# A hybrid decoder block on one core: queries loaded ahead, gate products dealt first and last, the residual through the weight tiles, the query projection in one block

## The chip, the cores and the metric

One core of a Trainium2 chip. The metric is the device time of one execution in microseconds (us); lower is better. The kernel before was timed three times.

## The reference, cut to what matters

All of it in float32: one sequence of 1024 tokens, width 1024, one layer.

```
h = rms_norm(x); proj = h @ w_in                      # q | six k/v parts | branch gates | pool input | merge gates
a = nsa_attention(q, kv, gates, ...) @ w_branch_attn   # compressed blocks, selected blocks, sliding window
b = pool_mixer(u_pool) @ w_branch_pool
ga, gb = split(sigmoid(g_merge))
x = x + (ga * a + gb * b) @ w_out                      # residual
x = x + square(relu(rms_norm(x) @ w_ff1)) @ w_ff2
return rms_norm(x)
```

With 16 selected blocks of 64 out of 16, the selected branch is plain causal attention. Eight heads of 64 in two groups share keys and values.

## The kernel before, in words

Every float32 matrix product is made of three products in TensorE's reduced float32 form: each operand is split into a high part (a cast on ScalarE, `hi`) and a low part (a subtraction on VectorE or GpSimd, `lo`), and `mm3` (lines 74 to 79) runs hi by hi, hi by lo and lo by hi for each block of 128 of the sum. A "term" below is one such triple.

`load` (lines 164 to 183) brings weights: a DMA on the SP queue into a raw tile `wraw` (four slots, `RAWS`), a cast to `whi` and a subtraction to `wlo` (three slots each, `HILO`), or, when a pool `blk` is given, into `bhi` and `blo`, which stay for a whole block of work.

The framework orders each engine's instructions itself ahead of time, by program order and by when it reckons that operands are there; on the chip each engine runs its list in that order. A pool that is opened where another was closed reuses its memory, and its tiles wait until the old ones are no longer read.

The stages, in program order:

1. Keys and values of the first parts (lines 229 to 271).
2. `block2` and `compress` (lines 286 to 384, called in lines 405 to 411): the rest of the keys and values, and the compressed blocks; `X`, `Xh`, `Xl` are the work tiles of `compress`.
3. `qblock(0)` and `qblock(1)` (lines 386 to 403): queries, 256 columns each, for eight tiles of 128 tokens. Each result is copied twice side by side by ScalarE (`q`, two slots), rotated by GpSimd (`rope`), and written to DRAM (`qd`). `keys` (lines 358 to 366) rotates and transposes keys in between, with `rope` on VectorE; both use the buffers `ropeA` and `ropeB` (two slots each).
4. The pool mixer and its gate `gb` (lines 424 to 505). Its weights' low parts are made by GpSimd. GpSimd also issues large DMAs that add weight blocks in DRAM for the MLP (`weight_sums`).
5. Attention (lines 511 to 744): 32 pairs of heads and token tiles (i from 0 to 7, four head pairs each). `units_a` is scores and softmax of a pair, `units_b` transposes the probabilities (`tr`) and multiplies them with the values (`pv`); they are interleaved, the `units_b` of one pair with the `units_a` of the next. The compressed values `vch` have 64 rows, all others (`vst`) 128. Between them, `advance` (lines 689 to 694) deals out 128 terms of the gate projection `ga` (`ga_terms`, PSUM tile `psG`), in proportion to the work done: `given < nterm * done / total`. The queries are read back from `qd` by `load_q` (lines 541 to 544) into `qi`, and transposed and split by `split_q`.
6. The merge (lines 787 to 825), in two halves of 512 tokens: for eight blocks, the attention branch's projection times `ta` (the gate from stage 5) plus `gb`, both read from DRAM; then eight blocks of `w_out`. The residual `xT` is written by DMA straight into `acc[:, m, sl]` (line 817), and line 820 adds to it.
7. The MLP with the norms (lines 829 to 984).

Of the kernel before, what the change touches and what calls it, by code (L numbers as in the profile page):

```python
# [49 lines left out]
def build(tc, a, out, dbg=None):  # L50
# [87 lines left out]

    def rope(eng, v, nh, cos, sin, wk):
        cb = cos[:, None, None, :].to_broadcast([P, nh, 2, 8])  # L140
        sb = sin[:, None, :].to_broadcast([P, nh, 8])
        A = wk.tile([P, 8, 2, 8], F32, name="ropeA", bufs=2)[:, :nh]
        B = wk.tile([P, 8, 2, 8], F32, name="ropeB", bufs=2)[:, :nh]
        x = v[:, :, 0:16].rearrange("p h (b e) -> p h b e", b=2)
        eng.tensor_tensor(A, x, cb, op=MUL)
        eng.tensor_tensor(B[:, :, 0], x[:, :, 1], sb, op=MUL)
        eng.tensor_tensor(B[:, :, 1], x[:, :, 0], sb, op=MUL)
        eng.tensor_tensor(x[:, :, 0], A[:, :, 0], B[:, :, 0], op=SUB)
        eng.tensor_tensor(x[:, :, 1], A[:, :, 1], B[:, :, 1], op=ADD)

# [13 lines left out]
    def load(src, lo_eng=None, blk=None):  # L164
# [3 lines left out]
        for a0 in range(0, na, step):  # L168
            w = step * n
            raw = strm.tile([P, HALF], F32, tag="wraw", name="wraw", bufs=RAWS)  # L170
            if blk is None:
                hi = strm.tile([P, HALF], F32R, tag="whi", name="whi", bufs=HILO)
                lo = strm.tile([P, HALF], F32R, tag="wlo", name="wlo", bufs=HILO)
            else:
                hi = blk.tile([P, 280], F32R, tag="bhi", name="bhi", bufs=10)
                lo = blk.tile([P, 280], F32R, tag="blo", name="blo", bufs=10)
            v, h, l = raw[:, :w], hi[:, :w], lo[:, :w]
            nc.sync.dma_start(v.rearrange("p (a n) -> p a n", a=step), src[:, a0:a0 + step, :])
            nc.scalar.copy(h, v)  # L179
            sub(lo_eng or nc.gpsimd, l, v, h)  # L180
            his.append(h.rearrange("p (a n) -> p a n", a=step))
            los.append(l.rearrange("p (a n) -> p a n", a=step))
# [4 lines left out]
    vst = [vk.tile([P, NT, NG, P], F32R, name=f"vst{b}") for b in range(2)]  # L187
    vch = vk.tile([DH, NG, P], F32R, name="vch")
    kds = vk.tile([P, NG, NCB + S], F32R, name="kds")
# [91 lines left out]
    with ExitStack() as st:  # L281
        psF = pool(st, "psF", bufs=4, space=PSUM)
        psH = pool(st, "psH", bufs=2, space=PSUM)
        wkA = pool(st, "wkA", side="right")

        def compress(kv):
            X = wkA.tile([P, 16, NG, NCB], F32, name="X")
            Xh = wkA.tile([P, 16, NG, NCB], F32R, name="Xh")
            Xl = wkA.tile([P, 16, NG, NCB], F32R, name="Xl")
            nc.gpsimd.memset(X[DH:P, :, :, NCB - 1:NCB], 0.0)  # L290
# [57 lines left out]
            else:  # L348
# [6 lines left out]
                for g in range(NG):  # L355
                    nc.vector.tensor_copy(vch[:, g], f(vh[g * DH:(g + 1) * DH]))

# [27 lines left out]

        def qblock(b):
            w = block_w(b * 256, 256)
            for t in range(NT):
                sl = slice(t * P, (t + 1) * P)
                ps = psF.tile([P, HALF], F32, name="psF")  # L390
                mm3(ps[:, :256], [(XH[k][:, sl], XL[k][:, sl], w[0][:, k], w[1][:, k])
                                  for k in range(NK)])
                q = wkA.tile([P, 4, 2, DH], F32, name="q", bufs=2)
                nc.scalar.activation(q, dup(ps[:, :256].rearrange("p (h d) -> p h d", d=DH)), AF.Copy,
                                     scale=req[:, t:t + 1])
                rope(nc.gpsimd, q.rearrange("p h e d -> p (h e) d"), 8, cosT[:, t], sinT[:, t], wkA)
                nc.sync.dma_start(qd[t][:, b * 512:(b + 1) * 512], q.rearrange("p h e d -> p (h e d)"))
                if b == 0:
                    keys(t, 0, kds[:, :, NCB + t * P:NCB + (t + 1) * P])
                elif t in (2, 5):  # L400
                    hf = t // 3
                    bcast(rB[:, hf * HALF:(hf + 1) * HALF], rcol[:, 4 * hf:4 * hf + 4],
                          psH.tile([P, HALF], F32, name="psH"), wkA)
# [7 lines left out]
        nc.vector.tensor_scalar(sg, sg, 0.5, 0.5, op0=MUL, op1=ADD)  # L411
        qblock(0)
        qblock(1)
        dump("kds", f(kds))
# [5 lines left out]
    kvctx.close()  # L420
    blkctx.close()


    with ExitStack() as st:
# [6 lines left out]
        with ExitStack() as st2:  # L431
# [45 lines left out]
            for m in (3, 2, 1, 0):  # L477
                cur = pool_in(m)
                if prev is not None:
                    pool_mix(*prev)  # L480
                prev = cur
            for m in range(NK):
                if made:
# [27 lines left out]
    with ExitStack() as st:  # L511
# [13 lines left out]
        def ga_terms():  # L525
            for m in range(NK):
                gh, gl = load(cols(a["w_in"], C_GA + m * P, P))
                for hf in range(2):
# [10 lines left out]
                    yield  # L539

        def load_q(i, g):
            qi = wk.tile([P, HALF], F32, name="qi", bufs=2)
            nc.sync.dma_start(qi, qd[i][:, g * HALF:(g + 1) * HALF])
            return qi

# [90 lines left out]
        def units_b(u):  # L636
            i, hp, g, nw, w0 = (u[n] for n in ("i", "hp", "g", "nw", "w0"))
            blocks = [(u["pS"], NCB + b * P, vst[0][:, b, g], P) for b in range(i + 1)]
            blocks += [(u["pW"], b * P, vst[1][:, w0 + b, g], P) for b in range(nw // P)]
            blocks.append((u["pS"], 0, vch[:, g], NCB))  # L640
            o = oacc[:, hp % 2]
# [4 lines left out]
            def tr(gi):  # L646
                bl = groups[gi]
                n = len(bl)
                ps = psT.tile([P, HALF], F32, name="psT").rearrange("p (b e n) -> p b e n", b=2, e=2)
                for j, (src, c0, _, _) in enumerate(bl):  # L650
                    for e in range(2):
# [7 lines left out]
            def pv(gi):  # L659
                ph, pl = parts.pop(gi)  # L660
                for part in (ph, pl):
                    for j, (_, _, v, rows) in enumerate(groups[gi]):
                        nc.tensor.matmul(o, lhsT=v, rhs=part[:rows, j], start=gi == 0 and j == 0 and part is ph,  # L663
                                         stop=2 * gi + j == nb - 1 and part is pl)
# [16 lines left out]

        LAG = 1
        fill = ga_terms()
        pairs = [(i, hp) for i in range(NT) for hp in range(NH // 2)]
        weight = [min(i + 1, 5) + i + 2 for i, _ in pairs]
        total, nterm = sum(weight), 2 * NK * NK
        done, given, summed = 0.0, 0, 0

        def advance(w):
            nonlocal done, given  # L690
            done += w
            while given < nterm and given < nterm * done / total:
                next(fill, None)
                given += 1

        qi = load_q(0, 0)
        q = split_q(qi)
        qnext = load_q(0, 1)
        bseq, bw = [], 0
# [42 lines left out]
        dump("oT", oT)  # L742
    psTctx.close()
    attn.close()

# [41 lines left out]
    with ExitStack() as st:  # L787
        wm = pool(st, "wm")
        for hf in range(2):
# [25 lines left out]
            for m in range(NK):  # L815
                wh, wl = load(cols(a["w_out"], m * P, P), nc.vector)
                nc.sync.dma_start(acc[:, m, sl], a["xT"][m * P:(m + 1) * P, sl])
                ps = bank()
                mm3(ps, [(wh[:, k], wl[:, k], mg[k][0], mg[k][1]) for k in range(NK)])
                nc.vector.scalar_tensor_tensor(acc[:, m, sl], ps, 0.5, acc[:, m, sl], op0=MUL, op1=ADD)  # L820
                square_into(sqs, acc[:, m, sl], m == NK - 1, sqa)
# [222 lines left out]
```

## Time and profile before

| | |
|---|---|
| median of 3 runs | 1493.94 us (1491.46 to 1497.39) |
| the profiled execution | 1493.06 us |
| its span, first to last instruction | 1491.3 us |
| TensorE busy | 1443.1 us (97%) |
| VectorE busy | 1006.1 us (67%) |
| ScalarE busy | 759.2 us (51%) |
| GpSimd busy | 154.1 us (10%) |

The profile is one execution. Times in it run from the span's start. Busy shares are of the span. A TensorE product is listed with its start and its own length; products overlap, so that the distance from one start to the next is what a product costs in a row of them.

### The profile page before, as it was taken

The page shows a single profiled execution, that of the slowest core. Times are in us where ns is not written, and L with a number is a line of the kernel's source. Part 1 is how long each engine was busy: PE and PEld are TensorE (multiplying, and loading weights), DVE is VectorE, ACT ScalarE, POOL GpSimd, SP SyncE. Part 2 cuts the span into 40 slices and gives each one's busy share as a digit, 9 for nine tenths or more (in the row PEclk, how much of TensorE's full clock was granted, in tenths as well). Part 3 has the DMA queues.
Part 4 walks back from the last instruction along what each step waited for, and adds up shares of the span by engine and source line. Part 5 has one row for each costly group of instructions (what it writes and reads, how often), then busy time and mean ns, then how long its engine had stood idle before and what let it go on. Part 6 is the DMA issues. An engine that isn't in the chain of part 4 may idle for free.

```text
span 1491.3 us, 20797 instructions
## 1 busy us (share of the span) xinstructions
PE 1443.1 (97%) x7385; PEld 1193.7 (80%) x7385; DVE 1006.1 (67%) x1950; ACT 759.2 (51%) x1559; POOL 154.1 (10%) x214
## 2 busy tenths in 40 slices
PE   8899999998999999999899999999999999999996
PEld 6788888886778887787688888888888888888885
DVE  5793461115888888787657658667897376669995
ACT  4454231124778877776334454575344454764451
POOL 2006423331111111111000000000000000000000
PEclk9999999999999999999999999999999999999998
DMA  8234217875768678766955332333233233333323
GB/s 309 69 100 149 71 43 189 215 202 132 201 156 212 153 187 196 171 169 150 327 174 162 108 97 91 100 100 99 85 106 97 94 99 93 99 94 97 98 80 113
DMA packets 130233, 204.67 MB, mean 137 GB/s; under 512 B 9936, under 2 KB 62928, under 8 KB 129616
## 3 DMA queue, kind: packets, MB, share of 16 engines
q1 hardware_dynamic: 112064, 136.22, 29.7%
q0 software_dynamic: 17920, 67.11, 19.9%
q8 instruction: 58, 0.95, 0.2%
q14 instruction: 47, 0.39, 0.1%
q10 hardware_dynamic: 144, 0.00, 0.0%
HBM read 186.52 MB, written 83.89 MB: 181 GB/s over the span
## 4 chain that ended last, share of the span: by engine, by line
PE 87%; DVE 5%; DMA 3%; ACT 2%; issue 1%; POOL 0%; SPq 0%; DVEq 0%; ACTq 0%; POOLq 0%
PE psm L79 16%; PE psm L77 16%; PE psm L78 16%; PE oacc L663 6%; PE psF L78 5%; PE psF L79 5%; PE psF L77 5%; PE psT L652 4%; PE psS L557 3%; PE psS L558 2%; PE psG L77 2%; PE psG L78 2%; PE psG L79 2%; DMA gb<-gbd 1%; PE psS L560 1%
## 5 line engine op out<-in xcount | busy, mean ns | idle before, releaser
L77 PE MATMUL psm<-mv,whi 128*128 128x512 f32 x896 | 350.6, 391 | 0.0
L78 PE MATMUL psm<-mv,whi 128*128 128x512 f32 x896 | 350.6, 391 | 0.0
L79 PE MATMUL psm<-mv,wlo 128*128 128x512 f32 x896 | 350.5, 391 | 0.0
L866 ACT CAST whi<-wraw 128x512 fp32r<-128x512 f32 x224 | 138.9, 621 | 257.6 <-PE psm L78 193.0
L82 DVE TENSOR_TENSOR wlo<-wraw,whi 128x512 fp32r<-128x512 f32 x288 | 196.7, 686 | 90.7 <-ACT whi L866 70.0
L78 PEld LDWEIGHTS psm<-mv,whi 128*128 128x128 f32 x896 | 168.3, 188 | 36.8
L77 PEld LDWEIGHTS psm<-mv,whi 128*128 128x128 f32 x896 | 168.3, 188 | 36.7
L79 PEld LDWEIGHTS psm<-mv,wlo 128*128 128x128 f32 x896 | 168.3, 188 | 36.7
L179 ACT CAST whi<-wraw 128x512 fp32r<-128x512 f32 x112 | 69.7, 622 | 122.2 <-PE psF L78 57.9
L656 DVE TENSOR_TENSOR pl<-psT,ph 128x512 fp32r<-128x512 f32 (+1 forms) x160 | 101.9, 646 | 30.3 <-ACT ph L655 29.0
L655 ACT CAST ph<-psT 128x512 fp32r<-128x512 f32 (+1 forms) x160 | 87.7, 556 | 49.4 <-PE psT L652 47.6
L567 DVE TENSOR_REDUCE nm<-psS 128x1 f32<-128x64 f32 (+8 forms) x192 | 99.8, 539 | 17.4 <-PE psS L560 10.2
L82 POOL TENSOR_TENSOR wlo<-wraw,whi 128x512 fp32r<-128x512 f32 x48 | 65.5, 1367 | 120.3 <-ACT whi L179 100.0
L77 PE MATMUL psF<-xh,whi 128*128 128x512 f32 x192 | 74.7, 389 | 0.0
L78 PE MATMUL psF<-xl,whi 128*128 128x512 f32 x192 | 74.7, 389 | 0.0
L79 PE MATMUL psF<-xh,wlo 128*128 128x512 f32 x192 | 74.7, 389 | 0.0
L568 ACT ACTIVATE pS<-psS,nm 128x64 f32<-128x64 f32 (+8 forms) x128 | 67.9, 532 | 8.8 <-DVE nm L567 8.3
L846 ACT CAST mv<-mt 128x512 fp32r<-128x512 f32 x96 | 59.1, 617 | 15.9 <-DVE mt L844 11.4
L82 DVE TENSOR_TENSOR mv<-mt,mv 128x512 fp32r<-128x512 f32 x96 | 65.0, 684 | 1.1 <-ACT mv L846 0.6
L663 PE MATMUL oacc<-ph,vst 128*128 128x256 f32 x264 | 64.0, 317 | 1.2 <-ACT ph L655 0.9
L652 PE MATMUL psT<-cf,pS 128*128 128x128 f32 x352 | 60.5, 276 | 2.7 <-DVE pS L624 2.6
L77 PE MATMUL psF<-bhi,xh 128*128 128x256 f32 (+1 forms) x192 | 55.6, 293 | 5.7 <-DVE vst L270 4.4
(248 smaller groups left out, 2970.0 us busy)
## 6 DMA issues: line engine op xcount, KB each, us to landing
wraw<-wsw_ff SPq DMA_DIRECT2D x128, 256.0 KB
wraw<-in_w_ff SPq DMA_DIRECT2D x96, 256.0 KB
wsw_ff<-in_w_ff POOLq DMA_DIRECT2D x16, 1024.0 KB, 9.1
wsw_ff<-wsw_ff POOLq DMA_DIRECT2D x16, 1024.0 KB, 9.5
wraw<-in_w_in SPq DMA_DIRECT2D x40, 256.0 KB
wraw<-in_w_out SPq DMA_DIRECT2D x32, 256.0 KB
xt<-in_x SPq DMA_DIRECT2D x8, 512.0 KB
qd<-q SPq DMA_DIRECT2D x16, 256.0 KB
```

Source lines behind the costliest of these rows:

```text
L77: nc.tensor.matmul(ps, lhsT=sh, rhs=mh, start=first and i == 0, stop=False, skip_group_check=more)
L78: nc.tensor.matmul(ps, lhsT=sh, rhs=ml, start=False, stop=False, skip_group_check=more)
L79: nc.tensor.matmul(ps, lhsT=sl, rhs=mh, start=False, stop=last and i == n - 1, skip_group_check=more)
L82: eng.tensor_tensor(lo, src, f(hi), op=SUB)
L179: nc.scalar.copy(h, v)
L567: nc.vector.tensor_reduce(nm, v, axis=AX.X if flat else AX.XY, op=MAX, negate=True)
L568: nc.scalar.activation(p if flat else p.rearrange("p (a n) -> p a n", a=2), v, AF.Exp, bias=nm, accum_out=sm)
L652: nc.tensor.transpose(ps[:, j, e], src[e][:, c0:c0 + P], ident)
L655: nc.scalar.copy(ph[:, :n], ps[:, :n])
L656: nc.vector.tensor_tensor(pl[:, :n], ps[:, :n], f(ph[:, :n]), op=SUB)
L663: nc.tensor.matmul(o, lhsT=v, rhs=part[:rows, j], start=gi == 0 and j == 0 and part is ph, stop=2 * gi + j == nb - 1 and part is pl)
L866: nc.scalar.copy(hi, raw)
```

## The change

Six edits:

- `rope` gets a tag, so that the rotation of the queries (GpSimd) and that of the keys (VectorE) have buffers of their own.
- `vch` has 128 rows, the lower 64 of them zero, and `pv` multiplies all 128 rows of the probabilities with it.
- `X`, `Xh`, `Xl` get a pool that is closed ahead of the queries, and in its place comes a pool `qb` for the query weights.
- `qblock` runs once, with 512 columns: seven of eight weight blocks in `qb`, the eighth in the shared `whi`/`wlo`.
- `qi` gets a pool of its own that is open from stage 4 on; its first two tiles are loaded ahead of the loop over the gate `gb`.
- `advance` deals 20 gate terms at once, 92 in proportion to the work, and 16 at the end (0.4 of them in each of the last two passes, the rest behind the loop).
- The residual is read into a `wraw` tile and added from there.

```diff
-    def rope(eng, v, nh, cos, sin, wk):
+    def rope(eng, v, nh, cos, sin, wk, tag=""):
-        A = wk.tile([P, 8, 2, 8], F32, name="ropeA", bufs=2)[:, :nh]
-        B = wk.tile([P, 8, 2, 8], F32, name="ropeB", bufs=2)[:, :nh]
+        A = wk.tile([P, 8, 2, 8], F32, name="ropeA" + tag, bufs=2)[:, :nh]
+        B = wk.tile([P, 8, 2, 8], F32, name="ropeB" + tag, bufs=2)[:, :nh]
...
-                hi = blk.tile([P, 280], F32R, tag="bhi", name="bhi", bufs=10)
-                lo = blk.tile([P, 280], F32R, tag="blo", name="blo", bufs=10)
+                hi = blk.tile([P, n], F32R, tag="bhi", name="bhi", bufs=8 if n < HALF else 7)
+                lo = blk.tile([P, n], F32R, tag="blo", name="blo", bufs=8 if n < HALF else 7)
...
-    vch = vk.tile([DH, NG, P], F32R, name="vch")
+    vch = vk.tile([P, NG, P], F32R, name="vch")
+    nc.gpsimd.memset(f(vch[DH:P]), 0.0)
...
+        xctx = ExitStack()
+        xp = pool(xctx, "xp", side="right")
-            X = wkA.tile([P, 16, NG, NCB], F32, name="X")
+            X = xp.tile([P, 16, NG, NCB], F32, name="X")
...
-                    nc.vector.tensor_copy(vch[:, g], f(vh[g * DH:(g + 1) * DH]))
+                    nc.vector.tensor_copy(vch[0:DH, g], f(vh[g * DH:(g + 1) * DH]))
...
-        def qblock(b):
-            w = block_w(b * 256, 256)
+        def qblock():
+            w7 = load(cols(a["w_in"], C_Q, HALF, 0, 7), nc.vector, qb)
+            w1 = load(cols(a["w_in"], C_Q, HALF, 7, 1), nc.vector)
+            w = [Parts(w7[e].tiles + w1[e].tiles) for e in range(2)]
             for t in range(NT):
-                mm3(ps[:, :256], [(XH[k][:, sl], XL[k][:, sl], w[0][:, k], w[1][:, k])
-                                  for k in range(NK)])
+                mm3(ps, [(XH[k][:, sl], XL[k][:, sl], w[0][:, k], w[1][:, k]) for k in range(NK)])
+                for b in range(2):
+                    q = wkA.tile([P, 4, 2, DH], F32, name="q", bufs=2)
+                    nc.scalar.activation(q, dup(ps[:, b * 256:(b + 1) * 256].rearrange("p (h d) -> p h d", d=DH)),
+                                         AF.Copy, scale=req[:, t:t + 1])
+                    rope(nc.gpsimd, q.rearrange("p h e d -> p (h e) d"), 8, cosT[:, t], sinT[:, t], wkA, "q")
+                    nc.sync.dma_start(qd[t][:, b * 512:(b + 1) * 512], q.rearrange("p h e d -> p (h e d)"))
-                if b == 0:
-                    keys(t, 0, kds[:, :, NCB + t * P:NCB + (t + 1) * P])
-                elif t in (2, 5):
+                keys(t, 0, kds[:, :, NCB + t * P:NCB + (t + 1) * P])
+                if t in (2, 5):
...
-        qblock(0)
-        qblock(1)
+        xctx.close()
+        qb = pool(st, "qb", side="right")
+        qblock()
...
+    qctx = ExitStack()
+    qp = pool(qctx, "qp")
+    def load_q(i, g):
+        qi = qp.tile([P, HALF], F32, name="qi", bufs=2)
+        nc.sync.dma_start(qi, qd[i][:, g * HALF:(g + 1) * HALF])
...
+            qi = [load_q(0, 0), load_q(0, 1)]
             for m in range(NK):
                 if made:
                     next(sums)
...
-                        nc.tensor.matmul(o, lhsT=v, rhs=part[:rows, j], start=gi == 0 and j == 0 and part is ph,
+                        nc.tensor.matmul(o, lhsT=v, rhs=part[:, j], start=gi == 0 and j == 0 and part is ph,
...
-        LAG = 1
+        LAG, FIRST, LAST = 1, 20, 16
...
             done += w
-            while given < nterm and given < nterm * done / total:
+            if len(bseq) and n >= len(pairs) - 1:
+                ending += 0.4 * LAST / nslot
+            while given < nterm and given < FIRST + (nterm - FIRST - LAST) * done / total + ending:
                 next(fill, None)
...
-                nc.sync.dma_start(acc[:, m, sl], a["xT"][m * P:(m + 1) * P, sl])
+                xt = strm.tile([P, HALF], F32, tag="wraw", name="wraw", bufs=RAWS)
+                nc.sync.dma_start(xt, a["xT"][m * P:(m + 1) * P, sl])
...
-                nc.vector.scalar_tensor_tensor(acc[:, m, sl], ps, 0.5, acc[:, m, sl], op0=MUL, op1=ADD)
+                nc.vector.scalar_tensor_tensor(acc[:, m, sl], ps, 0.5, xt, op0=MUL, op1=ADD)
```

## Rows read from the trace of the kernel before

**Rows 1.** Windows: length, busy us (instructions) by engine, TensorE clock, DMA share, GB/s.

```profile
55.00:112.00 57.00, 52.96 (x385) 49.64 (x386) 48.06 (x147) 28.95 (x77) 1.09 (x3) 0.97 0.23 67
...
104.10:158.35 54.25, 50.60 (x413) 48.84 (x411) 21.21 (x93) 23.16 (x55) 28.41 (x78) 1.00 0.43 132
...
339.50:420.00 80.50, 70.74 (x433) 55.45 (x433) 58.14 (x192) 56.17 (x191) 10.21 (x11) 0.96 0.66 163
420.00:680.00 260.00, 258.00 (x1695) 211.03 (x1694) 210.75 (x449) 196.88 (x463) 42.97 (x48) 1.00 0.76 179
...
705.80:739.65 33.85, 26.50 (x97) 20.21 (x97) 19.47 (x33) 10.52 (x19) 1.53 (x2) 0.90 1.08 317
```

**Rows 2.** Timeline of TensorE, 156 to 162 us: start, length, line, operands, shape.

```profile
157.64 0.28 PE L77 MATMUL psF<-bhi,xh 128*128 128x256 f32 x1
157.99 0.28 PE L77 MATMUL psF<-bhi,xh 128*128 128x256 f32 x1
...
160.43 0.39 PE L77 MATMUL psF<-xh,whi 128*128 128x512 f32 x1
...
161.12 0.39 PE L77 MATMUL psF<-xh,whi 128*128 128x512 f32 x1
```

**Rows 3.** Waits of TensorE, 50 to 172 us: total us, times, longest.

```profile
PE psT L362 <- DVE kvA L149: 2.8, 6, 1.0
```

**Rows 4.** Timeline of GpSimd: first and last instruction of one query rotation.

```profile
115.06 0.45 POOL L145 TENSOR_TENSOR ropeA<-q,cf 128x128 f32<-128x128 f32 x1
...
116.42 0.32 POOL L149 TENSOR_TENSOR q<-ropeA,ropeB 128x64 f32<-128x64 f32 x1
```

**Rows 5.** Timeline of TensorE: products with `vch`, and their neighbours.

```profile
358.57 0.38 PE L663 MATMUL oacc<-ph,vch 64*128 64x256 f32 x1
...
483.60 0.39 PE L663 MATMUL oacc<-pl,vst 128*128 128x256 f32 x2
483.92 0.39 PE L663 MATMUL oacc<-ph,vch 64*128 64x256 f32 x1
484.15 0.28 PE L663 MATMUL oacc<-pl,vch 64*128 64x256 f32 x1
484.35 0.50 PE L77 MATMUL psG<-xh,whi 128*128 128x512 f32 x1
484.69 0.39 PE L78 MATMUL psG<-xl,whi 128*128 128x512 f32 x1
...
547.26 0.38 PE L663 MATMUL oacc<-ph,vch 64*128 64x256 f32 x1
547.58 0.50 PE L77 MATMUL psG<-xh,whi 128*128 128x512 f32 x1
547.91 0.39 PE L78 MATMUL psG<-xl,whi 128*128 128x512 f32 x1
...
705.58 0.38 PE L663 MATMUL oacc<-pl,vch 64*128 64x256 f32 x1
```

**Rows 6.** Groups by line, 420 to 680 us: count, busy us, mean ns, idle before.

```profile
L77 PE MATMUL psG<-xh,whi 128*128 128x512 f32 x91 | 38.9, 427 | 0.0
```

**Rows 7.** Timeline of TensorE, start of attention, with the idle before it.

```profile
346.65 0.90 PE L549 MATMUL psT<-cf,qi 128*128 128x128 f32 x4 [4.02 <-DMA qi<-qd]
```

**Rows 8.** DMA, 705.8 to 739.65 us: bytes and issues.

```profile
DMA packets 7538, 10.74 MB, mean 317 GB/s; under 512 B 512, under 2 KB 3567, under 8 KB 7520
...
accx<-in_xT SPq DMA_DIRECT2D x8, 256.0 KB
```

**Rows 9.** Chain that ended last, three of its DMAs: start, us, what.

```profile
132.01 3.24 DMA wraw<-in_w_in
...
720.80 8.78 DMA gb<-gbd
...
730.80 5.05 DMA wraw<-in_w_out
```

**Rows 10.** Page, costliest groups: one cast of a weight tile.

```profile
L179 ACT CAST whi<-wraw 128x512 fp32r<-128x512 f32 x112 | 69.7, 622 | 122.2 <-PE psF L78 57.9
```

More of the change, by code (lines that the diff above doesn't have):

```diff
@@ L284, in build @@
         wkA = pool(st, "wkA", side="right")
+        xctx = ExitStack()
+        xp = pool(xctx, "xp", side="right")
         def compress(kv):
-            X = wkA.tile([P, 16, NG, NCB], F32, name="X")
-            Xh = wkA.tile([P, 16, NG, NCB], F32R, name="Xh")
-            Xl = wkA.tile([P, 16, NG, NCB], F32R, name="Xl")
+            X = xp.tile([P, 16, NG, NCB], F32, name="X")
+            Xh = xp.tile([P, 16, NG, NCB], F32R, name="Xh")
+            Xl = xp.tile([P, 16, NG, NCB], F32R, name="Xl")
             nc.gpsimd.memset(X[DH:P, :, :, NCB - 1:NCB], 0.0)
@@ L390, in qblock @@
                 ps = psF.tile([P, HALF], F32, name="psF")
-                mm3(ps[:, :256], [(XH[k][:, sl], XL[k][:, sl], w[0][:, k], w[1][:, k])
-                                  for k in range(NK)])
[L393 to L397, printed above, removed]
-                if b == 0:
-                    keys(t, 0, kds[:, :, NCB + t * P:NCB + (t + 1) * P])
-                elif t in (2, 5):
+                mm3(ps, [(XH[k][:, sl], XL[k][:, sl], w[0][:, k], w[1][:, k]) for k in range(NK)])
[7 more added lines that the diff above has]
+                if t in (2, 5):
                     hf = t // 3
@@ L421, in build @@
     blkctx.close()
+    qctx = ExitStack()
[3 more added lines that the diff above has]
+        nc.sync.dma_start(qi, qd[i][:, g * HALF:(g + 1) * HALF])
+        return qi
     with ExitStack() as st:
@@ L539, in ga_terms @@
                     yield
[L541 to L544, printed above, removed]
         def split_q(qi):
@@ L637, in units_b @@
             i, hp, g, nw, w0 = (u[n] for n in ("i", "hp", "g", "nw", "w0"))
-            blocks = [(u["pS"], NCB + b * P, vst[0][:, b, g], P) for b in range(i + 1)]
-            blocks += [(u["pW"], b * P, vst[1][:, w0 + b, g], P) for b in range(nw // P)]
-            blocks.append((u["pS"], 0, vch[:, g], NCB))
+            blocks = [(u["pS"], NCB + b * P, vst[0][:, b, g]) for b in range(i + 1)]
+            blocks += [(u["pW"], b * P, vst[1][:, w0 + b, g]) for b in range(nw // P)]
+            blocks.append((u["pS"], 0, vch[:, g]))
             o = oacc[:, hp % 2]
@@ L649, in tr @@
                 ps = psT.tile([P, HALF], F32, name="psT").rearrange("p (b e n) -> p b e n", b=2, e=2)
-                for j, (src, c0, _, _) in enumerate(bl):
+                for j, (src, c0, _) in enumerate(bl):
                     for e in range(2):
@@ L661, in pv @@
                 for part in (ph, pl):
-                    for j, (_, _, v, rows) in enumerate(groups[gi]):
-                        nc.tensor.matmul(o, lhsT=v, rhs=part[:rows, j], start=gi == 0 and j == 0 and part is ph,
+                    for j, (_, _, v) in enumerate(groups[gi]):
+                        nc.tensor.matmul(o, lhsT=v, rhs=part[:, j], start=gi == 0 and j == 0 and part is ph,
                                          stop=2 * gi + j == nb - 1 and part is pl)
@@ L686, in build @@
         total, nterm = sum(weight), 2 * NK * NK
-        done, given, summed = 0.0, 0, 0
+        done, given, summed, ending = 0.0, 0, 0, 0.0
         def advance(w):
-            nonlocal done, given
+            nonlocal done, given, ending
             done += w
-            while given < nterm and given < nterm * done / total:
+            if len(bseq) and n >= len(pairs) - 1:
+                ending += 0.4 * LAST / nslot
+            while given < nterm and given < FIRST + (nterm - FIRST - LAST) * done / total + ending:
                 next(fill, None)
                 given += 1
-        qi = load_q(0, 0)
-        q = split_q(qi)
-        qnext = load_q(0, 1)
+        q = split_q(qi[0])
+        qnext = qi[1]
         bseq, bw = [], 0
@@ L743, in build @@
     psTctx.close()
+    qctx.close()
     attn.close()
```

## The prediction

> **What bounds the kernel now.** I read the windows first, then the waits and the timeline of the stages that the diff touches. In the dense part of attention TensorE is busy 258.00 of 260.00 us, VectorE 210.75 and ScalarE 196.88 [rows 1]: TensorE sets the pace, so there only fewer or cheaper products pay. It has idle time in three places that the change touches. Query projection: 50.60 busy of 54.25 us. Start of attention: 70.74 of 80.50, that is 9.8 us idle, of which the first product on the queries waits 4.02 us for the read of `qi` [rows 1, 7]. Merge of the first half: 26.50 of 33.85 us, with the DMA engines at 1.08 of their time and 317 GB/s [rows 1]. A product's own length says little, since products overlap; I price by the step from start to start: three 256-column products in 0.35 us, so 0.117 us each, and three 512-column ones in 0.69, so 0.23 each [rows 2].
>
> **A. Query projection in one block.** Before, 8 tiles × 8 weight blocks × 3 products × 2 halves = 384 steps × 0.117 = 44.8 us; after, 192 × 0.23 = 44.2 us. The products save 0.6 us and no more. The stage takes 54.25 us [rows 1], so 54.25 − 44.8 = 9.5 us go into transposes, sums, a changed clock and waits. Waits that the change ends: 2.8 us in 6 waits of a transpose for the rotation of keys on VectorE, which shares `ropeA`/`ropeB` with GpSimd [rows 3]; and the second loading of eight blocks. I take −5 us, between −1 (0.6 and little else) and −9.5 (all of it). What is added: the new `qb` tiles need the memory of `X`, which is released only after `compress`; their loads on SP stand behind that, and TensorE behind the loads. With `block2` for seven tiles in between (7 × 24 × about 0.12 = 20 us), that is hidden; bare, it costs one landing, 3.24 us [rows 9]. The eighth block holds one of three `whi`/`wlo` through the stage, and `pool_in`'s two tiles fit the other two; uncovered, again one landing. On GpSimd the last query tile now leaves two rotations of about 1.7 us (115.06 to 116.74) [rows 4] ahead of the low parts that `pool_in` needs: up to 3.4 us, if those stand behind them. These ends lie inside −1. The writes of `qd` on SP stay 16 of the same size. The memset on GpSimd comes before its first real work: nothing, at worst its own length, under one rotation.
>
> **B. `vch` with 128 rows.** Twice the rows are no more columns, so a price change must come from how TensorE switches between 64 and 128 rows. Rows show such a price: a `vch` pair from 483.60 (two `vst` products) to 484.69 takes 1.09 us over four 256-column steps and one of 512; 4 × 0.117 + 0.23 = 0.70, excess 0.39. A single one, 547.26 to 547.91, takes 0.65 for 0.117 + 0.23 = 0.35, excess 0.30 [rows 5]. There are 64 `vch` products from 358.57 to 705.58, in 46 groups: 18 pairs and 28 alone. After 420 us lie 12 pairs and 22 alone: 12 × 0.39 + 22 × 0.30 = 11.3 us, in a stretch where TensorE never waits, so all of it counts. Before 420 lie 6 pairs and 6 alone, 4.1 us; part of it hides beside waits there, so I count half, 2. Together −13.3; ends −11.3 and −15.4, and 0 if the excess belongs to the place and not to the rows.
>
> This is where a page speaks against the change. The Trainium skill, "TensorE: Matmul & The Clock Gate", section "LDWEIGHTS (loading the stationary operand)", says that a load of weights takes a time set by its columns and not by its rows ("A 32×128 weight load takes the same time as a 128×128 weight load"). By that rule B would be 0 and the sum 13 us higher; the rows above do not exclude it, since they show an excess beside 64-row products and not its cause.
>
> **C. 20 gate terms first, 16 last.** A term is 3 × 0.23 = 0.69 us. Dealt in proportion, the pairs of i = 0 to 2 (weights 60 of 296) get 26 of 128 terms up to 420 us; 91 lie in the dense part [rows 6]; 11 are left. After, the dense part gets 92 × 0.71, about 65, 26 fewer: 26 × 0.69 = 18 us less there, and the same 18 us more at the start and the end. Moving work is worth nothing in itself. It pays where TensorE idles: at the start, between 4.0 us (the wait for `qi`, which goes if the two loads stand ahead of the `gb` loop, and whose place the first terms would fill anyway) and 9.8 us (all idle time to 420) [rows 1, 7]. I take −7.5, past the middle, as both the loads and the terms act there. The early loads are two DMAs on SP; before them in its list stand writes of queries that ended long ago, behind them weight loads, so nothing queues behind a wait.
>
> What is late next: VectorE. The dense part shrinks from 260 to 260 − 18 − 11.3 = 230.7 us, and VectorE's 210.75 us stay: 91%, and ScalarE's 85%, where it was 81% and 76%. No row shows this stretch at 91%. The nearest is 55 to 112 us, where VectorE was busy 48.06 of 57.00 (84%) and TensorE idled 4.04 of 57, 7%, against 0.8% in the dense part [rows 1]. 6 to 7% of 230.7 less those 2 us would be some 13 us; it is another stage with tighter chains, so I take +9. Ends: 0, and +29.3, at which VectorE's pace has swallowed all that TensorE saved there.
>
> **D. Merge.** The first half takes 33.85 us for 97 products [rows 1], 96 of 512 columns, 96 × 0.23 = 22.1: 11.75 us lost. The DMA engines are full, 10.74 MB, and among it are eight residual reads of 256 KB, which have no buffer to wait for and so run ahead of the `gb` and `ta` reads that the products need [rows 8]; the read of `gb` on the chain takes 8.78 us [rows 9]. In the changed kernel they must wait for a `wraw` slot and so come block by block with `w_out`. If six of eight go out of the stage, 6 × 0.26 = 1.6 MB at 317 GB/s = 5.0 us. The last gate terms cover about 1 us of the gap between attention and merge. −6; ends −1 (bytes only shift, something else in the merge is late) and −11.75.
>
> **Sum.** −5 −13.3 −7.5 +9 −6 = −22.8; 1493.06 − 22.8 = 1470.3. The profiled execution lies 0.9 us under the median, well inside the three runs' spread, so I forecast **1470** us.
>
> **The rivals.**
> 1. **VectorE takes over the dense part.** For it: 91%. Against: 84% cost only 7% elsewhere, and the parts' work is interleaved here. Then +29.3 stands for +9: 1470.3 + 20.3, about 1490.
> 2. **The 64-row excess belongs to the place**, for instance to the turn from products of `pv` to those of the gate, and stays. For it: the group's last excess can't be told from a turn, since a gate product follows. Then 1470 + 13 = 1483. Against it: in the pair at 483.92 the second product follows a 64-row one 0.23 us later, not 0.117 [rows 5], without a turn.
> 3. **Slower: the residual blocks the weight slots.** `wraw` has four slots, and in the `w_out` loop weights (two per block) and residual tiles now take them in turn. A residual tile is free only when its block's last addition is done, so a weight tile of block m+1 waits for the addition of block m−1. One block of products is 24 × 0.23 = 5.5 us; off that go the addition, the next weights' cast and subtraction, about three of 0.62 us [rows 10], so some 3.5 us are left for a landing. With a landing of 3.24 it costs nothing; with 5.05 [rows 9], 14 blocks × 1.55 = 22 us, the whole gain: 1492; from 5.7 us, 14 × 2.2 = 31, it is slower than before by over 0.5% (1501); with 8.78, 14 × 5.3 = 74: 1544. For it: 5.05 is a `w_out` landing. Against: it landed while the residual reads crowded the queues, and those are what is removed. Its time here: 1505 and up.
> 4. **Nothing is given back**: the +9 is 0 and the merge gains 9 for 6, with a little more at the start: about 1455.
> 5. **The change doesn't do what it says.** The framework orders each engine's list itself; it may put the first 20 terms where TensorE has work anyway, or the loads of `qi` no earlier. Then the 7.5 go: 1478.
>
> **How the numbers follow.** Forecast 1470, its own span 1458 to 1481: 0.56. Rival 1 (1482 to 1497) 0.13, rival 2 (1478 to 1488) 0.08, rival 3 (slower, or nearly the same) 0.06, rival 4 (1446 to 1458) 0.12, rival 5 (1474 to 1484) 0.05. For 8 in 10 the range takes the forecast, rivals 2 and 5, half of 4 and a part of 1: **1452 to 1488**. About 0.5% (7.5 us) is what a measurement here can tell from no change: faster means under 1486.5, slower over 1501.4. Most of rival 1 and some of 3 lie between: faster 0.86, same 0.09, slower 0.05.
>
> **What would show each step.** A: 192 products of 512 columns, no wait of transposes for L149, and a stage of about 49 us. B: `vch` products 128x256 and the next product 0.12 us after them, in pairs and alone; if 0.2 to 0.3 stays, rival 2. C: no DMA wait at the first product on `qi`, over 26 gate terms before attention is a quarter done, TensorE's idle share and VectorE's share in the dense part: over 8% idle is rival 1, under 2% rival 4. D: no `accx` read in the merge, fewer bytes there, and idle before TensorE in the `w_out` loop put down to `wraw` or `whi` if rival 3 holds. The prediction as a whole is wrong if TensorE's idle in the dense part grows by more than B and C save, or if a stage that the diff does not touch, such as the pool mixer, loses time because TensorE arrives earlier than its data.

## The result, and the profile after

The changed kernel takes 1481.03 us (median of 4 runs, 1480.51 to 1484.03) beside 1493.16 for the kernel before on the same chip: ratio 0.9919, interval 0.9894 to 0.9944. That is 12 us less; 1470 was forecast, in a range of 1452 to 1488. So the sign and the range hold, and half of the forecast gain is missing. The profiled execution has a span of 1479.3 us.

Stage by stage, in us (worked out from the timelines of both kernels; i is the token tile of attention). The stages of attention after i=0 begin with the first scores of their tile; the query projection, i=0, the merge and the last norm begin with the start of the last TensorE product of the stage before them:

| | start | query projection | pool mixer, gate | i=0 | i=1 | i=2 to 5 | i=6 | i=7 to end | merge, first half | to MLP | MLP | last norm |
|---|---|---|---|---|---|---|---|---|---|---|---|---|
| before | 104.0 | 54.3 | 180.9 | 31.9 | 29.1 | 176.1 | 59.3 | 69.8 | 34.1 | 113.2 | 619.6 | 9.0 |
| after | 102.4 | 49.6 | 181.2 | 33.0 | 29.4 | 172.0 | 58.0 | 69.0 | 31.4 | 113.3 | 619.6 | 10.6 |

The start has nothing in it that was changed for speed; over all kernels below it lies between 101.3 and 104.8, so a difference of some 2 us between two kernels says nothing by itself. The stage times are steadier, but for i=7 to the end and the merge, of which more below.

Windows of the changed kernel; columns as in [rows 1]. The lines answer to query projection, i=0, i=1, i=2 to 5, i=6, i=7 to end, and merge:

```profile
102.45:152.00 49.55, 49.32 (x225) 38.35 (x223) 21.17 (x85) 19.18 (x44) 25.24 (x72) 1.00 0.44 138
333.20:366.30 33.10, 29.93 (x177) 24.27 (x176) 18.48 (x68) 18.69 (x71) 5.41 (x5) 1.00 0.54 135
366.30:395.70 29.40, 27.80 (x185) 22.56 (x184) 25.86 (x80) 24.00 (x80) 4.66 (x5) 1.00 0.81 196
395.70:567.70 172.00, 169.24 (x1148) 138.98 (x1146) 145.65 (x338) 138.90 (x346) 29.09 (x33) 1.00 0.76 185
567.70:625.70 58.00, 56.71 (x381) 46.09 (x379) 48.91 (x98) 43.40 (x97) 9.56 (x10) 1.00 0.83 187
625.70:694.95 69.25, 64.26 (x406) 53.82 (x405) 51.74 (x98) 46.70 (x98) 8.20 (x10) 0.93 0.67 156
694.95:726.05 31.10, 26.03 (x97) 20.65 (x97) 19.52 (x32) 10.02 (x18) 1.53 (x2) 0.86 0.96 269
```

What to see: in the query projection TensorE is now busy 49.32 of 49.55 us. At i=0 it is far busier than before, yet the tile is not shorter. From i=7 to the end it is busy 64.26 of 69.25 us at a granted clock of 0.93, in a stretch where the kernel before had it busy for 69.89 of 70.20. The merge is still the least busy.

Gate products (`psG`, three to a term) in the same five stretches of attention, before, after, and in the first experiment that matters (a_even, below): length, busy time and count on TensorE, then its weight loads and VectorE:

```profile
339.30:371.20 31.90, 11.31 (x30) 6.12 (x30) 0.69 (x1) 0.89 0.51 132
371.20:400.30 29.10, 13.71 (x41) 7.04 (x41) 0.69 (x1) 1.00 0.74 188
400.30:576.40 176.10, 57.41 (x179) 30.20 (x179) 5.45 (x8) 1.00 0.76 182
576.40:635.70 59.30, 17.42 (x51) 8.57 (x51) 1.36 (x2) 1.00 0.81 181
635.70:705.90 70.20, 25.95 (x83) 13.74 (x83) 2.74 (x4) 1.00 0.67 159
```

```profile
333.20:366.30 33.10, 18.66 (x74) 13.40 (x74) 2.06 (x3) 1.00 0.54 135
366.30:395.70 29.40, 13.79 (x44) 7.42 (x43) 0.68 (x1) 1.00 0.81 196
395.70:567.70 172.00, 56.96 (x181) 30.62 (x181) 5.45 (x8) 1.00 0.76 185
567.70:625.70 58.00, 16.46 (x50) 8.39 (x50) 1.36 (x2) 1.00 0.83 187
625.70:694.95 69.25, 10.74 (x36) 6.25 (x36) 1.38 (x2) 0.93 0.67 156
```

```profile
335.30:357.20 21.90, 7.38 (x20) 3.51 (x20) 0.00 (x0) 1.00 0.65 160
357.20:384.70 27.50, 10.01 (x29) 5.40 (x28) 0.98 (x2) 0.94 0.70 179
384.70:560.10 175.40, 58.45 (x183) 30.76 (x183) 5.16 (x8) 0.99 0.76 180
560.10:620.60 60.50, 22.63 (x69) 11.34 (x69) 2.05 (x3) 1.00 0.77 185
620.60:689.00 68.40, 26.10 (x84) 13.96 (x84) 2.60 (x4) 1.00 0.72 171
```

The change was to thin out the dense part. It did not: from i=2 to 5 there are 181 gate products for 179. What went to the start came from the end, 36 for 83; and the last one of all runs at 664.97 us, 30 us before attention ends (before: at 704.04, 1.5 us before the last product of attention). The framework, which orders each engine's list itself, drew later terms forward, the sixteen "last" ones too.

### The profile page after: what moved, and what is told of

Same layout as the page of the kernel before. It is cut to its first block, busy times and chain, and to the rows that moved or that the text cites. A ratio compares the mean times of both kernels' runs of the same rounds, so it can differ in the third digit from the quotient of the medians.

```text
span 1479.3 us, 20379 instructions
## 1 busy us (share of the span) xinstructions
PE 1436.1 (97%) x7193; PEld 1183.8 (80%) x7193; DVE 1009.9 (68%) x1942; ACT 757.9 (51%) x1551; POOL 155.9 (11%) x215
## 4 chain that ended last, share of the span: by engine, by line
PE 84%; DVE 7%; DMA 3%; ACT 2%; POOL 2%; issue 2%; SPq 0%; DVEq 0%; POOLq 0%; ACTq 0%
PE psm L79 17%; PE psm L78 16%; PE psm L77 16%; PE oacc L672 5%; PE psT L661 4%; PE psF L78 4%; PE psF L77 4%; PE psF L79 4%; PE psS L566 3%; PE psS L567 2%; PE psG L77 2%; PE psG L78 2%; PE psG L79 2%; DMA ta<-tad 1%; PE psS L569 1%
## 5 line engine op out<-in xcount | busy, mean ns | idle before, releaser
L665 DVE TENSOR_TENSOR pl<-psT,ph 128x512 fp32r<-128x512 f32 (+1 forms) x160 | 101.9, 647 | 29.5 <-ACT ph L664 28.5
L661 PE MATMUL psT<-cf,pS 128*128 128x128 f32 x352 | 63.5, 287 | 5.8 <-DVE pS L633 5.6
L672 PE MATMUL oacc<-ph,vst 128*128 128x256 f32 x264 | 66.8, 329 | 1.2 <-ACT ph L664 0.8
L672 PE MATMUL oacc<-pl,vst 128*128 128x256 f32 x264 | 58.2, 300 | 2.4 <-DVE pl L665 2.3
```

Of the source, the lines that this page charges most:

```text
L661: nc.tensor.transpose(ps[:, j, e], src[e][:, c0:c0 + P], ident)
L665: nc.vector.tensor_tensor(pl[:, :n], ps[:, :n], f(ph[:, :n]), op=SUB)
L672: nc.tensor.matmul(o, lhsT=v, rhs=part[:, j], start=gi == 0 and j == 0 and part is ph, stop=2 * gi + j == nb - 1 and part is pl)
```

## The experiments

In each, "a_" is the changed kernel with one edit or two, "b_" the kernel before with one. They ran in three series; the kernel before took 1493.77, 1492.48 and 1492.46 us in them, so a difference between kernels of two series is good to about 1 us. Attention's stages, as above:

| | us | i=0 | i=1 | i=2 to 5 | i=6 | i=7 to end | merge |
|---|---|---|---|---|---|---|---|
| b_vch | 1486.86 | 31.4 | 28.9 | 172.8 | 58.0 | 68.0 | 35.1 |
| a_vch64 | 1488.08 | 33.6 | 29.8 | 176.6 | 59.6 | 70.1 | 30.2 |
| a_even | 1474.02 | 21.9 | 27.5 | 175.5 | 60.4 | 68.2 | 31.8 |
| a_even_qlate | 1472.89 | 21.9 | 26.3 | 175.3 | 60.9 | 68.2 | 34.5 |
| a_even_qwk | 1480.02 | 31.5 | 28.7 | 172.1 | 58.1 | 68.0 | 33.1 |
| a_qlate | 1478.79 | 33.0 | 29.5 | 172.1 | 58.0 | 66.8 | 30.9 |
| a_qwk | 1485.56 | 40.0 | 27.0 | 172.1 | 58.0 | 68.0 | 31.2 |
| a_hold6 | 1475.85 | 33.0 | 29.6 | 169.9 | 58.9 | 65.4 | 30.3 |
| a_acc | 1480.94 | 33.0 | 29.8 | 172.3 | 58.2 | 68.9 | 31.9 |
| a_q256 | 1482.93 | 33.0 | 29.2 | 173.2 | 58.1 | 66.9 | 30.8 |
| a_sums | 1473.10 | 33.0 | 29.1 | 172.1 | 58.2 | 66.8 | 25.0 |
| a_even_sums | 1470.46 | 23.1 | 27.6 | 177.2 | 61.7 | 68.3 | 24.5 |

**b_vch: only the 128 rows.**

```diff
-    vch = vk.tile([DH, NG, P], F32R, name="vch")
+    vch = vk.tile([P, NG, P], F32R, name="vch")
+    nc.gpsimd.memset(f(vch[DH:P]), 0.0)
-            blocks.append((u["pS"], 0, vch[:, g], NCB))
+            blocks.append((u["pS"], 0, vch[:, g], P))
```

> The kernel before with only the 128-row vch. If the excess after 64-row products comes from the rows (step B): 1493.2 - 11 to 15, so 1478 to 1482, the next product 0.12 us after a vch product, and the stretch of i = 2 to 5 (176.1 us before) shorter by 5 to 7 us. If the excess belongs to the place (rival 2): 1493 within 2 us and the same steps of 0.2 to 0.3 us. A third view, from the trace of the changed kernel, where that stretch lost 4.1 us at the same number of gate products: the rows are the cause, but part of the time saved turns into waits for VectorE; then 1483 to 1487.

Measured: 1486.86 beside 1493.77, ratio 0.9953 (0.9936 to 0.9969), 6.9 us less. The same place as the pair of [rows 5], timeline of TensorE in b_vch:

```profile
482.92 0.40 PE L664 MATMUL oacc<-pl,vst 128*128 128x256 f32 x2
483.16 0.28 PE L664 MATMUL oacc<-ph,vch 128*128 128x256 f32 x1
483.27 0.28 PE L664 MATMUL oacc<-pl,vch 128*128 128x256 f32 x1
483.39 0.40 PE L77 MATMUL psG<-xh,whi 128*128 128x512 f32 x1
483.62 0.40 PE L78 MATMUL psG<-xl,whi 128*128 128x512 f32 x1
```

From 482.92 to 483.62 it is 0.70 us, where it was 1.09: the excess of 0.39 is gone to the last hundredth. So the rows were the cause. How, the weight loads show, before and then in b_vch (PEld is the load that goes with a product):

```profile
483.48 0.30 PEld L663 LDWEIGHTS oacc<-pl,vst 128*128 128x128 f32 x2
483.92 0.18 PEld L663 LDWEIGHTS oacc<-ph,vch 64*128 64x128 f32 x1
484.02 0.19 PEld L663 LDWEIGHTS oacc<-pl,vch 64*128 64x128 f32 x1
484.35 0.19 PEld L77 LDWEIGHTS psG<-xh,whi 128*128 128x128 f32 x1
```

```profile
483.04 0.19 PEld L664 LDWEIGHTS oacc<-ph,vch 128*128 128x128 f32 x1
483.16 0.19 PEld L664 LDWEIGHTS oacc<-pl,vch 128*128 128x128 f32 x1
483.28 0.19 PEld L77 LDWEIGHTS psG<-xh,whi 128*128 128x128 f32 x1
```

With 128 rows each load begins 0.11 to 0.12 us ahead of its product. At a turn between 64 and 128 rows it begins with its product (483.92 and 484.35 before, the starts of the products in [rows 5]): there it is not done ahead. The load itself is as long with 64 rows as with 128, 0.18 to 0.19 us. That is what the Trainium skill says ("TensorE: Matmul & The Clock Gate", "LDWEIGHTS (loading the stationary operand)"), and the trace agrees; that the change of rows costs nothing does not follow from it.

Why 6.9 and not 13.3: in attention TensorE runs the same list in the same order in both kernels, so the steps from start to start can be set side by side one by one. The steps from the product ahead of each `vch` group to the one behind it go from 28.9 to 17.7 us after 420 us, and from 10.5 to 7.4 ahead of that. It makes no difference what follows: the groups with a gate product behind them gain 0.36 us each, and so do the others. So the excess was the rows', in all places, 14.2 us together. But the other steps of attention grew, from 317.2 to 323.2 us, the largest by 0.79 and 0.58 us, just ahead of products that wait for `pS` and `pl`, which VectorE writes; TensorE's waits for these two go from 3.0 to 5.1 us. And the first scores came 1.1 us later after the start of i=0. Of the 14.2 us, 7.1 are left in attention. That is the third view of the expectation, though VectorE is named for only 2.1 of the 6.0 us; what makes the rest is not shown.

**a_vch64: the same part undone in the changed kernel** (`vch` of 64 rows, `part[:64, j]` for it).

> The changed kernel with vch of 64 rows, as before. b_vch alone gave 6.9 us of the 13.3 of step B. If that is what the rows are worth: 1487 to 1489. If the rest of the 13.3 was there but hidden in b_vch by the order of before: 1491 to 1495. If part was lost again in the changed kernel: 1483 to 1486.

Measured: 1488.08, ratio 0.9975 (0.9962 to 0.9988): 7.0 us more than the changed kernel. The part is worth 7 us in either. Here, too, the steps around the groups grow by more, 15.6 us, and the others shrink by 7.3.

**a_even: the gate terms in proportion, as before.**

```diff
-        LAG, FIRST, LAST = 1, 20, 16
+        LAG, FIRST, LAST = 1, 0, 0
```

> The changed kernel with the gate terms dealt in proportion, as before (no 20 first, no 16 last). In the changed trace the first stretch of attention took up 47 more products for 1.1 us, and the last two token tiles lost about as much, since no gate term was left after 665 us. If this account holds, undoing the dealing moves the total by no more than 3 us (1478 to 1484): the start gets longer by 5 to 9 us, the end shorter by 5 to 9. If the dealing is worth what step C put down for it (7.5 at the start, less 9 given back, of which part belongs to vch): the start loses, the dense part gains 4 to 9 evenly, not only at the end. If the dealing is a clear gain: over 1486.

Measured: 1474.02, ratio 0.9876 (0.9854 to 0.9899): 7 us faster than the changed kernel. None of the three expectations; the account "as much won at the start as lost at the end" falls. The windows above tell why. With 49 gate products at i=0 and 1 these tiles take 49.4 us, with 118 they take 62.4: 69 more products at 0.23 us are 15.9 us, and 13.0 of it is paid: TensorE's idle time in these two tiles is 4.8 us with the early terms and 5.6 without, so they filled almost none of it. From i=2 to 6 the changed kernel has 21 fewer than a_even, 4.8 us of work, and is 5.9 us shorter. At the end 84 products take 68.4 us and 36 take 69.25: 48 fewer, 11.0 us of work, and nothing is won. Waits of TensorE from i=7 to the end, changed kernel, then a_even, and a_even's window:

```profile
PE psT L661 <- DVE pS L633: 1.8, 3, 0.9
PE psS L566 <- ACT pS L577: 1.7, 1, 1.7
PE oacc L672 <- DVE pl L665: 0.9, 4, 0.2
PE oacc L672 <- ACT ph L664: 0.3, 1, 0.3
```

```profile
PE psS L566 <- ACT pS L577: 0.3, 1, 0.3
```

```profile
620.60:689.00 68.40, 67.98 (x454) 57.42 (x453) 52.78 (x101) 48.05 (x101) 9.20 (x11) 1.00 0.72 171
```

So the terms at the end are free. They stand in for waits for the softmax, 5.0 us idle for 0.4, and they keep the clock up: behind the last gate product TensorE is busy 4.1 of the next 7.0 us, and then the granted clock falls to the lower of its two levels (1.2 of 2.4 GHz) for part of the stretch (it is 0.50 from 684 to 689 us), 0.93 on average for 1.00. As an estimate, 7% of 69.25 us, 4.8 us, is what that costs; with the 4.6 us of idle time it is nearly the 11.0. At the start, after the queries had their own memory, the terms were not free.

**a_hold6: the early terms kept, the last six groups of eight terms held back** until a given pair's result is there.

```diff
                     ps = psG.tile([P, HALF], F32, name="psG")
+                    late = {10: 18, 11: 20, 12: 23, 13: 25, 14: 27, 15: 29}.get(2 * m + hf)
+                    if late is not None:
+                        i_, hp_ = divmod(late, 4)
+                        nc.vector.tensor_copy(ps[0:1, 0:1], oT[0:1, hp_, i_ * P:i_ * P + 1])
```

> The changed kernel, with the last six gate groups (of 16) held back: each waits for an attention result of a given pair (one more small copy on VectorE each), so that the last group begins at 98% of the planned products of attention instead of 87%. Theory 1, from a_even: the 20 early terms cost TensorE's time where they stand, but cost the same in the dense part; what is lost is the cover at the end, where no gate product was left after 665 us. Then this is worth as much as undoing the dealing: 1472 to 1476, with the last token tile and the end together about 67 us at six to seven groups more evenly spread, and the dense part shorter. Theory 2: the early terms themselves are dear (they delay the softmax of the first tiles): 1479 to 1482. Theory 3, step C as forecast (VectorE sets the pace once terms are gone): no change in the dense part, 1481.

Measured: 1475.85, ratio 0.9888 (0.9868 to 0.9908), 5.2 us faster than the changed kernel with the same 20 terms at the start. From i=7 to the end it is 3.6 us shorter, although 62 gate products now run there for 36: the waits are 1.7 us for 4.7, and the granted clock is 1.00 for 0.93. For the end this is theory 1. From i=2 to 6 it is not: there are 26 fewer gate products, 6.0 us of work, and the stretch is only 1.1 us shorter. Windows of i=2 to 5 and of i=6:

```profile
397.20:567.20 170.00, 165.16 (x1125) 135.52 (x1123) 144.28 (x334) 136.36 (x341) 27.37 (x31) 1.00 0.75 183
567.20:626.10 58.90, 56.41 (x376) 45.32 (x375) 50.14 (x104) 44.38 (x97) 9.77 (x10) 1.00 0.80 183
```

TensorE idles 7.3 us there, for 4.1 in the changed kernel. Against a_even 21 products went with 5.9 us, here 26 with 1.1: what a term costs in the dense part stays open. What the early terms cost at the start stays (33.0 and 29.6 us).

**a_qlate, a_even_qlate: the query loads back to their old place in the program**, with their own pool kept; once with the dealing of the changed kernel, once in proportion.

```diff
-            qi = [load_q(0, 0), load_q(0, 1)]
...
-        q = split_q(qi[0])
-        qnext = qi[1]
+        qi = load_q(0, 0)
+        q = split_q(qi)
+        qnext = load_q(0, 1)
```

> The changed kernel with the two query loads where they were before, ahead of the attention loop. If the early loads and the 20 early terms fill the same hole (theory 1): no loss, 1480 to 1483, since the terms cover the wait of 4.0 us; the first tile 33 to 35 us. If the early loads act by themselves whatever is dealt: 1485 to 1488 (+4 to +7).

> Gate terms dealt in proportion and the queries loaded late, all else as in the changed kernel. Against a_even (1474.0, first tile 21.9 us) this shows what the early loads are worth when nothing else covers the wait. Theory 1: the first tile goes back to 29 to 32 us, TensorE waits for the load of qi again; part comes back in the second tile; total 1479 to 1484. If the shorter first tile came from something else in the change: 1474 to 1476.

Measured: 1478.79 (0.9914, 0.9886 to 0.9942) and 1472.89 (0.9868, 0.9846 to 0.9890). The first tile keeps its 33.0 and 21.9 us. So the place of the loads in the program does nothing: with the tile's memory free, the framework issues the first two loads of `qi` within the query projection wherever they are written. SyncE's timeline, changed kernel, a_even_qlate, and the kernel before, where the first load comes only at the end of the gate:

```profile
121.03 1.11 SPq L433 DMA_DIRECT2D qi<-qd  x2
```

```profile
121.52 1.30 SPq L433 DMA_DIRECT2D qi<-qd  x2
```

```profile
339.68 0.34 SPq L543 DMA_DIRECT2D qi<-qd  x1
```

The 2.2 us that a_qlate gains on the changed kernel lie from i=7 to the end (66.8 for 69.0), with the same products and a granted clock of 0.97 for 0.93; they are not the edit's.

**a_even_qwk, a_qwk: the query tiles back in attention's work pool**, whose memory the pool mixer still reads, and loaded late; again in proportion, and with 20 terms first.

```diff
-        qi = qp.tile([P, HALF], F32, name="qi", bufs=2)
+            qi = wk.tile([P, HALF], F32, name="qi", bufs=2)
```

> As a_even_qlate, and the query tiles back in the work pool of attention, as before, whose memory the pool mixer uses until its last product. a_even_qlate kept the short first tile (21.9 us), so the place of the loads in the program is not what shortened it. If it is the memory of their own: the read of qi waits again for the end of the pool mixer, TensorE waits some 4 us for it, the first tile is 29 to 32 us and the total 1479 to 1483. If it is neither: 21.9 us and 1473 to 1475.

> The changed kernel (20 terms first, 16 last) with the query tiles in the work pool and loaded late, as before. With a_even, a_even_qwk and the changed kernel this makes four: terms early or even, query tiles with their own memory or not. If terms and memory fill the same hole: no loss here, first tile 33 to 35 us and 1479 to 1483. If the memory is worth the same 6 to 9 us in both: 1486 to 1490.

Measured: 1480.02 (0.9924, 0.9903 to 0.9944) and 1485.56 (0.9953, 0.9938 to 0.9968). The wait is back in both; first product on the queries, a_even_qwk and then a_qwk:

```profile
341.14 0.66 PE L554 MATMUL psT<-cf,qi 128*128 128x128 f32 x4 [4.06 <-DMA qi<-qd]
```

```profile
340.20 1.11 PE L554 MATMUL psT<-cf,qi 128*128 128x128 f32 x4 [4.57 <-DMA qi<-qd]
```

With that there are four kernels. Own memory gives 6.0 us with even dealing (1480.02 to 1474.02) and 4.5 with early terms (1485.56 to 1481.03); early terms cost 7.0 and 5.5. The two do not fill the same hole: even where TensorE waits for `qi`, the early terms don't cover it, because all but eight products of them stand behind the queries' transposes in its list, as with even dealing.

**a_acc: the residual straight into `acc`**, as before.

```diff
-                nc.sync.dma_start(xt, a["xT"][m * P:(m + 1) * P, sl])
+                nc.sync.dma_start(acc[:, m, sl], a["xT"][m * P:(m + 1) * P, sl])
```

> The changed kernel with the residual read straight into acc, as before. The merge of the first half took 33.85 us before and 31.10 after. If the residual reads were what held it: 1484 (+2.7), and the merge is 33 to 35 us again. Step D forecast +6: 1487. If something else shortened it (the last gate term, which ended before the end of attention, and its write): 1481 within 1.5, merge about 31.

Measured: 1480.94, ratio 0.9926 (0.9903 to 0.9948): the same as the changed kernel. Windows of its merge, to be read against 31.10 us, 0.96 and 269 GB/s above:

```profile
696.60:728.30 31.70, 26.14 (x98) 20.66 (x98) 19.64 (x33) 10.02 (x18) 1.53 (x2) 0.85 1.02 294
```

The reads come back (0.96 MB more in the stretch), and the stage is 0.6 us longer. The residual was not what held it.

**a_sums: the weight sums of the MLP, which GpSimd adds in DRAM, dealt out faster.**

```diff
-            if n >= 2 and summed < 25 * done / total:
+            if n >= 2 and summed < 28 * done / total:
```

> The changed kernel with the weight sums in DRAM, which GpSimd issues, dealt out faster (28 for 25 over attention), so that fewer of them fall into the merge. a_acc left the time as it was, so the residual reads did not hold the merge. If the sums' traffic holds it (40% of the DMA engines' time there, against 55% for all reads of the SP queue): the merge goes from 30.0 us to 22 to 27 and the total to 1474 to 1478. If the reads of ta and gb are late because they may only be issued after attention's last result: 30 us and 1481.

Measured: 1473.10, ratio 0.9870 (0.9849 to 0.9891), 7.9 us faster than the changed kernel; the merge is 6.3 us shorter, and i=7 to the end 2.2, with the clock at 0.97 as in a_qlate. DMA queues in the merge (packets, MB, share of the 16 engines; q1 is SP's, q0 GpSimd's), changed kernel and then a_sums, and a_sums' window:

```profile
q1 hardware_dynamic: 4840, 5.46, 54.9%
q0 software_dynamic: 952, 2.87, 40.4%
```

```profile
q1 hardware_dynamic: 4949, 5.52, 70.0%
```

```profile
695.30:720.10 24.80, 23.70 (x98) 19.33 (x98) 19.93 (x34) 10.88 (x20) 0.00 (x0) 0.93 0.70 223
```

SP's bytes are nearly the same; without GpSimd's 2.87 MB the merge takes 24.8 us for 31.1.

**a_q256: the query projection in two blocks**, as before (`qblock(0)`, `qblock(1)`, shared rotation buffers).

> The changed kernel with the query projection in two blocks of 256 columns and shared rotation buffers, as before. By step A: +5, 1486, the stage 54 us for 49.6; by the lower bound of step A: +1, 1482. If the time gained there is lost again in the pool mixer or at the start of attention: 1481.

Measured: 1482.93, ratio 0.9939 (0.9920 to 0.9958). Its query stage:

```profile
101.30:155.80 54.50, 50.67 (x413) 48.92 (x413) 21.03 (x94) 23.27 (x55) 28.51 (x78) 1.00 0.43 131
```

The stage is 4.9 us longer, the whole only 1.9. In this profile the start was 1.1 us shorter and the stretch from i=7 to the end 2.1, neither of which the edit touches; the 2.1 go with a granted clock of 0.97 for 0.93 there. The pool mixer kept its 181.2 us. So I take 4.9 for the part, and the rest for that spread.

**a_even_sums: even dealing, and the sums still faster (30 for 25).** Two edits from above in one.

> The changed kernel with the gate terms dealt in proportion and the weight sums dealt out faster (30 for 25). If the two gains add (a_even -7.0, a_sums -7.9, both against the changed kernel): 1465 to 1468, the merge 22 to 25 us. If the sums' traffic in attention now delays its weight loads: attention over 356 us, and 1470 or more.

Measured: 1470.46, ratio 0.9854 (0.9840 to 0.9869), the fastest of all. The gains don't add (10.6 of 14.9): the merge has its 24.5 us, but attention is 357.9 us for 353.5. The first expectation holds for the merge, the second for attention.

## Why the prediction was right, and where it was not

**A, query projection (−5): right.** 54.3 to 49.6 us, and back to 54.5 in a_q256. The wait for the rotation [rows 3], 6 times and 2.8 us, is down to 0.3, and TensorE is busy all through the stage. Nothing of the added work showed: the stage behind it took 181.2 us for 180.9.

**B, `vch` (−13.3): the excess right, the sum not.** 7 us in both directions. The excess per group [rows 5] was no misreading: after 420 us the groups lost 11.2 us for the 11.3 put down, ahead of that 3.0 of 4.1. The step that failed is "a stretch where TensorE never waits, so all of it counts". The other steps of attention grew by 6.0 us, 2.1 of them waits for VectorE. Rival 2 (the place and not the rows) did not happen.

**C (−7.5 + 9): the sum nearly right, both terms for the wrong reason.** The own memory of the queries gives 4.5 to 6.0 us at the start; that is the term "idle at the start", within its bounds of 4.0 and 9.8, but neither the place of the loads in the program nor the early terms had a part in it: the memory alone did it. The give-back of 9 was put on VectorE in the dense part. There VectorE went to 145.65 of 172.00 us, 85%, for 83% before, and TensorE idled no more than before: rival 1 did not happen. It could not show, since the terms had not left; in a_hold6, where 26 products do leave, TensorE idles 3.3 us more, so a give-back is there, though which wait makes it is not shown. What was given back, 7.0 us, is the dealing itself: work moved from the end, where it cost nothing, to the start, where it did. The step that failed is "26 fewer terms in the dense part": the dealing fixes how early a term may come in the program, and the framework then drew the terms forward at the pace of before. That is rival 5, for the last terms rather than for the first ones, and it was forecast at 1478. That −7.5 + 9 comes so near the measured −6.0 + 7.0 is luck.

**D, merge (−6): failed.** The full DMA engines [rows 8] were read rightly, but not who filled them: the eight residual reads were picked out because the change removes them, while GpSimd's 3.08 MB in the same stretch were not looked at (DMA queues of the kernel before, 705.8 to 739.65 us):

```profile
q0 software_dynamic: 1056, 3.08, 40.6%
```

a_acc puts the residual at 0 in the total and 0.6 us in the stage, a_sums the weight sums at 6.3 in the stage. Why the merge still shrank by 2.7 us with the change stays open: over the kernels here that have the sums in it, it is 30.2 to 31.9 with the early terms and 31.8 to 35.1 with even dealing, and no run shows what in the dealing does it.

**Rival 3 (slots blocked by the residual): did not happen.** From the merge to the MLP it is 113.2 and 113.3 us, and TensorE waits for no weight in the `w_out` loop. **Rival 4** would have needed D.

The sum by what was measured: −4.9 −7.0 −6.0 +7.0 and about 0 for the residual make −10.9, with the 12 us of the total.

## What to carry to other kernels

Cover work is worth something only where TensorE would wait: look for the stretch in which removing it saves nothing, and leave it there. Where a framework orders the instructions, dealing them out in program order is a wish; a dependency, or memory that is free, is what moves them, so check in the trace where they ran. And when a full DMA stage is to be relieved, list all queues that load it before taking out the one that the change happens to touch.

## What the runs showed of the hardware that was not expected

The turn between 64-row and 128-row products costs 0.1 to 0.2 us each, because the weight load is not done ahead there; 64 more rows, of zeros, cost less than the turn.

From i=7 to the end the changed kernel and a_acc take 69.0 and 68.9 us at a granted clock of 0.93, and a_qlate, a_q256 and a_sums, with the same products there, 66.8 to 66.9 at 0.97. Two kernels can differ by 2 us in a stretch with waits that no edit touched; the granted clock of the stretch shows it.

The last norm has 32 one-column products, the same in all kernels. Timeline before, after and in a_acc:

```profile
1473.57 4.09 PE L768 MATMUL psm<-ones,sqd 128*128 128x1 f32 x32
```

```profile
1459.98 5.69 PE L779 MATMUL psm<-ones,sqd 128*128 128x1 f32 x32
```

```profile
1463.22 4.02 PE L779 MATMUL psm<-ones,sqd 128*128 128x1 f32 x32
```

They took 4.0 to 5.7 us, and the granted clock of the last norm was 0.72 before and 0.61 after, in fractions of the upper of its two levels (2.4 and 1.2 GHz): TensorE has little work there. No edit explains the 1.6 us by which the stage grew: a_qlate, which differs from the changed kernel only in where the query loads are written, takes 8.6 us for it where that takes 10.6.
